# One Strassen level in the down product, and a causal convolution as three half-length filters, in a hybrid decoder layer

## The chip, the cores and the metric

The kernel runs on one core of one Trainium2 chip. The metric is the device time of one execution in microseconds (us); the time before is the median of three runs.

A core has TensorE (PE in the profile; its weight loads are PEld), VectorE (DVE), ScalarE (ACT), GpSimd (POOL) and SyncE (SP), which here only issues DMA transfers. Each engine works through its own queue in a fixed order.

## What is computed

One decoder layer on 2048 tokens of 1024 channels. After a first projection, half of the channels go through a sparse attention and half through a causal depthwise convolution; their normalised outputs are mixed into h, and a SwiGLU network follows. In the reference, with what the change does not touch left out:

```python
D_MODEL, SEQ, CONV_CH, CONV_WIDTH, FFN_HIDDEN = 1024, 2048, 512, 31, 2816

def conformer_conv(u, w_dw, b_dw, ln_g, ln_b):
    a, gate = jnp.split(u, 2, axis=-1)
    hcv = a * jax.nn.sigmoid(gate)
    hcv = lax.conv_general_dilated(hcv, w_dw, window_strides=(1,), padding=[(CONV_WIDTH - 1, 0)],
                                   feature_group_count=CONV_CH) + b_dw
    ...

hn = rms_norm(x, ffn_norm_g[l])
g_ff, u_ff = jnp.split(hn @ w_gate_up[l], 2, axis=-1)
x = x + (jax.nn.silu(g_ff) * u_ff) @ w_down[l]
```

## The kernel before, in words

Large products are made in float16 with both operands split into a high and a low part, so that one logical product is three matmuls: high x high, high x low and low x high. A split takes ScalarE (scale and cast to the high part) and then VectorE (scale, subtract the high part, cast).

**Convolution.** In the first phase, `conv` (L441) makes the gated input `hc` of one block of 128 channels and 1024 tokens, with 30 tokens of the block before it ahead, and puts 31 taps on a list. There are 8 such convolutions (4 channel blocks x 2 halves of the tokens). `tap` (L307) takes one from the list: a tap is one VectorE operation on 128x1024 elements, the first L317, the others L320, and all 31 add into the same tile `acc`. `mm3`, which issues the matmuls of the projection, takes a tap each time that it has streamed PACE = 3600 columns, and makes the tap wait for that matmul; what is left is worked off at the end of the half.

**Gate-up.** `ffn` (L1209) does gate and up in one Strassen level of its own: for each half `b` of the tokens (1024 each) and each chunk `j` of 128 hidden channels (22 chunks), `up` makes 7 products of 12 matmuls, 128x128 by 128x512. The weights' combinations s1, s2, s3 (`sm`) are made on GpSimd (L1394, L1395, L1402, L1415) and split by `wsplit` (L1349, L1350); the operands from the tokens are made in the first step of a half (L1315, L1316, L1327, L1329, L1334). Each chunk has one scale: ScalarE squares its weights (`chunk_norm`, L1249), a small matmul sums over partitions, and `root` (L1262) takes the power on GpSimd. The results go through tanh (L1378, ScalarE), a product (L1379, VectorE) and a second product (L1380, GpSimd), are squared for the scale of the activations (L1369, ScalarE), and are stored to HBM by SyncE as `act`.

**Down.** Four blocks `tb` of 512 tokens are each multiplied by all of w_down: for each of the 22 chunks one activation tile and one weight tile of 512 KB are loaded, split in three pairs (L1462 and L1463 for the activations, L1467 and L1468 for the weights), and 4 x 2 x 3 matmuls (L1475 to L1477) add into 8 PSUM banks. At the end of a block VectorE adds the residual h (L1483) and SyncE stores.

The order of the work on each engine is set by a scheduler from the order of the code and the tiles' buffers; taps have a low priority.

Of the kernel before, what the change touches and what calls it, by code (L numbers as in the profile page):

```python
# [25 lines left out]
NJ = HID // 128  # L26
CW = 31
EPS = 1e-6
# [19 lines left out]
PACE = (3600, 3600, 3600, 3600)  # L48
# [14 lines left out]
TAP0 = 0  # L63
# [30 lines left out]
class Body:  # L94
# [25 lines left out]
    def scratch(self):  # L120
        for name, w in (("qkv", 1048), ("mixc", 512), ("hd", D)):
            setattr(self, name, [self.dr.tile([128, w], F32, name=f"{name}{i}") for i in range(NT)])
        self.xt = [self.dr.tile([128, KT, 512], F32, name=f"xt{i}") for i in range(4)]
        self.act = [self.dr.tile([128, T], F32, name=f"act{j}") for j in range(NJ)]

# [181 lines left out]
    def tap(self, after=None):  # L307
        nc = self.nc
        w, acc, hc, j = self.taps.pop(0)
        with self.tc.high_priority(-LOWP):  # L310
            if w == 0:
                b0 = self.col["conv_dw_b"] + j
                if TAP0:
                    i = nc.scalar.activation(acc, hc[:, 0:1024], AF.Identity, scale=self.wdw[:, 0, j:j + 1],
                                             bias=self.vec[:, b0:b0 + 1])
                else:
                    i = nc.vector.tensor_scalar(acc, hc[:, 0:1024], self.wdw[:, 0, j:j + 1], self.vec[:, b0:b0 + 1],  # L317
                                                op0=ALU.mult, op1=ALU.add)
            else:
                i = nc.vector.scalar_tensor_tensor(acc, hc[:, w:w + 1024], self.wdw[:, w, j:j + 1], acc,  # L320
                                                   op0=ALU.mult, op1=ALU.add)
        if after is not None:
            self.tc.add_manual_dep(i.ins, after.ins.name,
                                   mybir.DependencyInfo(mybir.DependencyClass.Sync, mybir.DependencyReason.DATA),
                                   reason="taps keep pace with the matrix products")

# [4 lines left out]
    def phase_A_body(self, pb, ctx, ctx0):  # L331
# [23 lines left out]
        halo = sa.tile([128, 4, CW - 1], F32, name="halo")  # L355
        nc.vector.memset(halo, 0.0)
        kct = s0.tile([128, 4, 8, 129], F32, name="kct")
# [83 lines left out]
        def conv(j, x2, w2, between):  # L441
            hc = sa.tile([128, 1024 + CW - 1], F32, name="hc", tag="hc", bufs=HCB)
            nc.vector.tensor_copy(hc[:, :CW - 1], halo[:, j, :])
            for h in range(2):
                p = colmm(0, x2[h], w2)
                between(2 * h)
                t = s0.tile([128, 512], F32, name="sg", tag="sg", bufs=1)
                nc.scalar.activation(t, p, AF.Tanh, scale=w2[3])
                p = colmm(128, x2[h], w2)
                between(2 * h + 1)  # L450
                hv = hc[:, CW - 1 + h * 512:CW - 1 + (h + 1) * 512]
                nc.scalar.activation(hv, p, AF.Copy, scale=w2[2])
                nc.vector.scalar_tensor_tensor(hv, t, 1.0, hv, op0=ALU.add, op1=ALU.mult)
            nc.vector.tensor_copy(halo[:, j, :], hc[:, 1024:])
            acc = sa.tile([128, 1024], F32, name="acc", tag="acc", bufs=4)
            for w in range(CW):
                self.taps.append((w, acc, hc, j))
# [751 lines left out]
    def ffn(self, last, close_c):  # L1209
        nc, tc, I = self.nc, self.tc, self.I  # L1210
        with ExitStack() as ctx:
            sb = ctx.enter_context(tc.tile_pool(name="sbF", bufs=1, reuse_waits="tile"))
            ps = ctx.enter_context(tc.tile_pool(name="psF", bufs=1, space=PSUM, reuse_waits="tile"))
            self.xp = (ps, "pt", 2)
            self.hpool, self.htag = sb, ("wr", 6, "ev", EVB)
            wsc = sb.tile([128, 3, NJ], F32, name="wsc")
            ass = sb.tile([128, 2, 2 * NJ], F32, name="ass")
            dss = sb.tile([128, NJ], F32, name="dss")
            fin = sb.tile([128, 8], F32, name="fin")
            ssum = sb.tile([128, 3], F32, name="ssum")  # L1220
            one = sb.tile([128, 1], F32, name="one")
            nc.vector.memset(one, 1.0)
            sac = sb.tile([128, 2, NJ], F32, name="sac")
# [22 lines left out]
            def chunk_norm(ws):  # L1246
                ss = sb.tile([128, 2], F32, name="css", tag="css", bufs=2)
# [4 lines left out]
            def root(s, cols, pool=False):  # L1252
                if pool:
                    nc.gpsimd.partition_all_reduce(cols, cols, 128, bass.bass_isa.ReduceOp.add)
# [298 lines left out]
```

## Time and profile before

| | |
|---|---|
| runs (us) | 2837.37, 2833.8, 2825.53; median 2833.8 |
| the profiled execution | 2831.96 us, of it the profile's span 2830.2 us |
| mean granted TensorE clock | 0.96 |
| TensorE / VectorE / ScalarE / GpSimd busy | 2544.5 / 2030.0 / 1468.4 / 1020.0 us |
| convolution and projection | about 0 to 700 us of the span |
| attention and mixing | about 700 to 1480 us |
| gate-up, first and second half of the tokens | about 1480 to 1940, 1940 to 2370 us |
| down | about 2358 to 2830 us |

The shares of busy time are averages over stages with different limits, so the table by stage and the waits of one stage tell more than the page's first section. The granted clock is a share of TensorE's full 2.4 GHz. A matmul's duration in the profile (379 ns at full clock) is longer than the distance between two starts, since matmuls are pipelined.

### The profile page before, as it was taken

How to read it: one execution, taken by the hardware profiler on the slowest of the kernel's cores; microseconds unless marked ns; L12 is line 12 of the kernel's file. 1: busy time of each engine (PE TensorE's matmuls, PEld its weight loads, DVE VectorE, ACT ScalarE, POOL GpSimd, SP SyncE). 2: the span in 40 equal slices, each digit the busy share in tenths (PEclk: the TensorE clock that was granted, in tenths of full speed). 3: DMA queues.
4: the chain of work that ended last, by engine and by line, in shares of the span. 5: the costliest groups of instructions: out<-in, count | busy, mean ns of one | idle time of the engine just before them, and what ended most of it. 6: DMA issues, size and time to landing. Idle time of an engine off the chain costs nothing. (4 is left out here: it accounts for less than half of the span.)

```text
span 2830.2 us, 46376 instructions
## 1 busy us (share of the span) xinstructions
PE 2544.5 (90%) x17692; PEld 1547.2 (55%) x17692; DVE 2030.0 (72%) x3291; ACT 1468.4 (52%) x3101; POOL 1020.0 (36%) x903
## 2 busy tenths in 40 slices
PE   6987977666889988999987999997999999999999
PEld 3476446545677777777873444443444444444444
DVE  4899798889999898988767666668655556444442
ACT  7434632477667665655565555555544445433331
POOL 1001354545444443333455545547444441000000
PEclk9999988878999999999998999999999999999999
DMA  6124221113211111000025323333433225466452
GB/s 214 53 79 132 69 62 53 56 54 109 67 63 48 44 46 32 31 28 28 27 72 179 101 79 97 113 104 123 138 118 93 81 88 191 144 215 218 153 172 67
DMA packets 236088, 271.76 MB, mean 96 GB/s; under 512 B 18192, under 2 KB 172232, under 8 KB 235864
## 3 DMA queue, kind: packets, MB, share of 16 engines
q1 hardware_dynamic: 235616, 268.70, 29.8%
q8 instruction: 138, 2.26, 0.3%
q14 instruction: 86, 0.70, 0.1%
q10 hardware_dynamic: 248, 0.09, 0.0%
HBM read 207.73 MB, written 61.01 MB: 95 GB/s over the span
## 5 line engine op out<-in xcount | busy, mean ns | idle before, releaser
L1357 PE MATMUL ps<-oph,wh 128*128 128x512 f16 x1232 | 469.7, 381 | 33.6 <-DVE u L1405 10.9
L1359 PE MATMUL ps<-oph,wl 128*128 128x512 f16 x1232 | 470.1, 382 | 3.9 <-DVE wl L1350 3.8
L1360 PE MATMUL ps<-opl,wh 128*128 128x512 f16 x1232 | 470.1, 382 | 2.1 <-DVE opl L1316 1.8
L320 DVE SCALAR_TENSOR_TENSOR acc<-hc,wdw,acc 128x1024 f32<-128x1024 f32 x240 | 330.1, 1388 | 10.6
L1056 ACT ACTIVATE mp<-s,few 128x512 f32<-128x512 f32 x412 | 269.2, 691 | 108.7 <-PE s L1048 74.6
L1066 POOL TENSOR_TENSOR mpl<-mp 128x512 f16<-128x512 f32 x206 | 228.8, 1113 | 238.6 <-ACT mp L1056 235.9
L1468 DVE SCALAR_TENSOR_TENSOR wl<-wr,fin,wh 128x512 f16<-128x512 f32 x176 | 126.6, 750 | 240.9 <-ACT wh L1467 240.7
L1006 DVE TENSOR_REDUCE bx<-pp 128x8 f32<-128x512 f32 (+1 forms) x426 | 274.8, 664 | 20.9 <-PE pp L1003 19.2
L1467 ACT ACTIVATE wh<-wr,fin 128x512 f16<-128x512 f32 x176 | 121.8, 719 | 275.2 <-PE pt L1476 273.9
L1359 PEld LDWEIGHTS <-wl 128*128 128x128 f16 x1232 | 120.9, 98 | 179.4 <-issue 35.3
L1046 PE MATMUL s<-r,k 128*128 128x256 f16 x824 | 211.4, 277 | 1.8 <-ACT mp L1056 1.3
L1048 PE MATMUL s<-r,k 100*128 100x256 f16 x824 | 212.3, 278 | 0.0
L1079 PE MATMUL uu<-v,mp 128*128 128x129 f16 x1648 | 205.5, 224 | 3.6 <-ACT us L1102 3.5
L1357 PEld LDWEIGHTS <-wh 128*128 128x128 f16 x1232 | 122.8, 100 | 156.8 <-ACT wh L1349 6.8
L1360 PEld LDWEIGHTS <-wh 128*128 128x128 f16 x1232 | 121.2, 98 | 146.7 <-issue 3.6
L1475 PE MATMUL ps<-wh,ah 128*128 128x512 f16 x528 | 200.1, 379 | 0.0
L1476 PE MATMUL ps<-wl,ah 128*128 128x512 f16 x528 | 200.1, 379 | 0.0
L1477 PE MATMUL ps<-wh,al 128*128 128x512 f16 x528 | 200.1, 379 | 0.0
L1079 PE MATMUL uu<-v,mpl 128*128 128x65 f16 x1648 | 189.6, 196 | 4.6 <-POOL mpl L1066 2.4
L1380 POOL TENSOR_TENSOR t<-t,c 128x512 f32<-128x512 f32 x88 | 142.5, 1620 | 120.1 <-DVE t L1379 110.6
L1066 DVE TENSOR_TENSOR mpl<-mp 128x512 f16<-128x512 f32 x206 | 162.9, 795 | 31.7 <-ACT mp L1056 31.2
L1003 PE MATMUL pp<-k,r 128*128 128x512 f16 (+3 forms) x544 | 163.0, 340 | 10.8 <-DVE bx L1006 9.0
(343 smaller groups left out, 6480.6 us busy)
## 6 DMA issues: line engine op xcount, KB each, us to landing
wr<-in_w_gate_up_dram SPq DMA_DIRECT2D x88, 512.0 KB, 3.8
wr<-in_w_down_dram SPq DMA_DIRECT2D x88, 512.0 KB, 4.4
act<-t SPq DMA_DIRECT2D x88, 256.0 KB, 2.1
a<-act SPq DMA_DIRECT2D x88, 256.0 KB, 5.4
raw<-in_w_in_dram SPq DMA_DIRECT2D x44, 256.0 KB, 3.9
wn<-in_w_down_dram SPq DMA_DIRECT2D x22, 512.0 KB, 3.6
x<-in_x_dram SPq DMA_DIRECT2D x16, 512.0 KB, 3.5
h<-in_x_dram SPq DMA_DIRECT2D x16, 512.0 KB, 3.7
```

Of the source, the lines that this page charges most:

```text
L320: i = nc.vector.scalar_tensor_tensor(acc, hc[:, w:w + 1024], self.wdw[:, w, j:j + 1], acc, op0=ALU.mult, op1=ALU.add)
L1006: nc.vector.tensor_reduce(bx[:, h0:h0 + per, 2 * (ka - k0):2 * (kb - k0)], mp.rearrange("p h (b x) -> p h b x", x=64), axis=AX.X, op=ALU.max)
L1046: nc.tensor.matmul(s[:, i], self.k1[br][:, g, ks], r1[:, h0:h0 + 2, :], start=i % 2 == 0, stop=False, skip_group_check=True)
L1048: nc.tensor.matmul(s[:, i], self.k2[br][:KAUG, g, ks], r2[:KAUG, h0:h0 + 2, :], start=False, stop=base is None, skip_group_check=True)
L1056: nc.scalar.activation(p32[:, :n], s[:, :n], AF.Exp, scale=self.kap[:, job[0][0]:job[0][0] + 1])
L1066: eng.tensor_tensor(pl[:, :n], p32[:, :n], ph[:, :n], op=ALU.subtract)
L1079: nc.tensor.matmul(uu[:, hh, :n], w[:, i, hh, :], self.v[br][:, self.slot(br, kt), g, :n], start=new, stop=last and n == 129, skip_group_c ...
L1357: nc.tensor.matmul(p, wh[:, k, :], xh[:, k, :], start=start and k == 0, stop=False, skip_group_check=True)
L1359: nc.tensor.matmul(p, wl[:, k, :], xh[:, k, :], start=False, stop=False, skip_group_check=True)
L1360: nc.tensor.matmul(p, wh[:, k, :], xl[:, k, :], start=False, stop=stop and k == 3, skip_group_check=True)
L1475: nc.tensor.matmul(p, ah[:, k, ts], ws[c][0], start=j == 0, stop=False)
L1476: nc.tensor.matmul(p, ah[:, k, ts], ws[c][1], start=False, stop=False)
```

## The change

**Down.** One Strassen level (Winograd's form): per half `b` of the tokens, w_down and the activations are cut in 2 x 2 blocks, 7 products of 11 k-steps x 4 row blocks x 3 matmuls are made, and sums of them give the four blocks of the output. The activations' sums S1 to S4 are made on GpSimd in gate-up (`combine`) and stored beside the blocks A11, A12 and A22. To that end gate-up walks its chunks in pairs (j, j + 11) that share one scale, with weights loaded two chunks ahead. The weights' sums T1 to T4 are made on GpSimd in `down` (`operand`), from float32 tiles that stay in SBUF for the half. The first three k-steps of the first product are split before gate-up ends (`early`). The last pair's stores go through GpSimd's queue (`store`), and the scale of the second half's activations is summed by a small matmul.

**Convolution.** Even and odd samples of `hc` are kept apart (read from PSUM with a stride of two). A filter of the even taps on the even samples (16 operations), one of the odd taps on the odd samples (15) and one of the summed taps on the summed samples (16) give the even outputs as the sum of the first two and the odd outputs as the third less both; 3 more operations make the sums. That is 50 operations on 512 to 527 elements in place of 31 on 1024. PACE is 2232 columns.

```diff
-PACE = (3600, 3600, 3600, 3600)
+PACE = (2232, 2232, 2232, 2232)
...
+        def even(i):
+            ev = tile("ev", 512) if i == 0 else t["ev"]
+            if i == 0:
+                return nc.vector.tensor_scalar(ev, x0[:, :512], h(0), self.vec[:, b0:b0 + 1], op0=ALU.mult, op1=ALU.add)
+            return stt(ev, x0[:, i:i + 512], h(2 * i), ev, op0=ALU.mult, op1=ALU.add)
...
+        def odd(i):
+            x = x1[:, i - 1:i + 512]
+            if i == 1:
+                return nc.vector.tensor_scalar(tile("fq", 513), x, h(1), None, op0=ALU.mult)
+            return stt(t["fq"], x, h(2 * i - 1), t["fq"], op0=ALU.mult, op1=ALU.add)
...
+        def cross(i):
+            x = t["fx"][:, i:i + 512]
+            if i == 0:
+                return stt(tile("od", 512), x, g(0), t["fp"], op0=ALU.mult, op1=ALU.subtract)
+            return stt(out[:, 1] if i == HALF else t["od"], x, g(i), t["od"], op0=ALU.mult, op1=ALU.add)
+
+        steps = [lambda i=i: even(i) for i in range(HALF + 1)] + [lambda i=i: odd(i) for i in range(1, HALF + 1)]
+        steps.append(lambda: tt(tile("fx", 512 + HALF), x0, x1, op=ALU.add))
+        steps.append(lambda: stt(tile("fp", 512), t["ev"], self.nb2[:, j:j + 1], t["fq"][:, 1:], op0=ALU.add, op1=ALU.add))
+        steps.append(lambda: tt(out[:, 0], t["ev"], t["fq"][:, :512], op=ALU.add))
+        return steps + [lambda i=i: cross(i) for i in range(HALF + 1)]
...
-                nc.scalar.activation(hv, p, AF.Copy, scale=w2[2])
+                hv = hc[:, :, HALF + h * 256:HALF + (h + 1) * 256]
+                nc.scalar.activation(hv, p.rearrange("p (m e) -> p e m", e=2), AF.Copy, scale=w2[2])
...
+            order = [j for i in range(NH2) for j in (i, i + NH2)]
+            ahead_w = [load_w(order[0]), load_w(order[1])]
             src = load_x(0)
...
-            chunk_scale(0, chunk_norm(nxt))
+            chunk_scale(0, chunk_norm(ahead_w[0] + ahead_w[1]))
...
+            def store(name, b, p, t):
+                last = b == 1 and p == NH2 - 1 and name not in ("A11", "S3")
+                (nc.gpsimd if last else nc.sync).dma_start(self.act[name][b][p], t)
+
+            def combine(b, j):
+                tt, p = nc.gpsimd.tensor_tensor, j % NH2
+                if j < NH2:
+                    a11, a21 = kept[j]
+                    s3 = at()
+                    tt(s3, a11, a21, op=ALU.subtract)
+                    store("S3", b, p, s3)
+                else:
+                    (a11, a21), (a12, a22) = kept.pop(p), kept.pop(j)
+                    tt(a21, a21, a22, op=ALU.add)
+                    store("S1", b, p, a21)
+                    tt(a11, a21, a11, op=ALU.subtract)
+                    store("S2", b, p, a11)
+                    s4 = at()
+                    tt(s4, a12, a11, op=ALU.subtract)
+                    store("S4", b, p, s4)
...
                 s3 = sm()
                 tt(s3, a11, a21, op=ALU.subtract)
+                flush(sums)
                 product(pb, wsplit(s3, j), src, ops, "T3", False, True)
...
+                if name == "T2":
+                    tt(b11, b12, b11, op=ALU.subtract)
+                    t2 = tile("t2", 3)
+                    tt(t2, b22, b11, op=ALU.subtract)
+                    return t2
...
+                if name == "T3":
+                    tt(b12, b22, b12, op=ALU.subtract)
+                    return b12
...
+                if name == "T4":
+                    t2 = tile("t2", 3)
+                    tt(t2, b22, b11, op=ALU.subtract)
+                    tt(b21, b21, t2, op=ALU.subtract)
+                    return b21
...
+            def product(p, a, name, start, stop):
+                for k in K:
+                    if b == 0 and a == "A11" and k < len(early):
+                        blocks[0, 0, k] = early[k][0]
+                        (ah, al), (wh, wl) = early[k][1:]
+                    else:
+                        x = tile("ar", 6)
+                        nc.sync.dma_start(x, self.act[a][b][k])
+                        ah, al = split("a", x, sac[:, b, k:k + 1])
+                        wh, wl = split("w", operand(name, k), sd)
+                    for i in range(4):
+                        ts = slice(i * 128, i * 128 + 128)
+                        s = start and k == 0
+                        nc.tensor.matmul(p[i], ah[:, ts], wh, start=s, stop=False, skip_group_check=True)
+                        nc.tensor.matmul(p[i], ah[:, ts], wl, start=False, stop=False, skip_group_check=True)
+                        nc.tensor.matmul(p[i], al[:, ts], wh, start=False, stop=stop and k == NH2 - 1,
+                                         skip_group_check=True)
...
+            product(pa, "A11", "B11", True, True)
...
+            if b == 0:
+                act_scale(root)
...
+            product(pb, "S2", "T2", True, True)
+            u2 = plus(pb, p1)
+            h = residual(0, 0)
+            product(pa, "A12", "B21", False, True)
+            result(0, 0, pa, h)
+            product(pb, "S3", "T3", False, True)
+            u3 = plus(pb, p1)
+            with_h(u3, 1, 1)
+            with_h(p1, 1, 0)
+            pc = [bank() for _ in range(4)]
+            product(pc, "S1", "T1", True, True)
+            result(1, 1, pc, u3)
+            with_h(u2, 0, 1)
+            product(pb, "A22", "T4", False, True)
+            result(1, 0, pb, p1)
+            product(pc, "S4", "B22", False, True)
+            result(0, 1, pc, u2)
```

The order of the instructions shows three places. The first is GpSimd's queue at the seam from gate-up to down. Before, the last products t*u (L1380) are followed only by the sum over partitions for the activation scale (ISA rows, then the power at L217), and GpSimd has no part in down:

```order
856 L1380 TENSOR_TENSOR t<-t,c_27531 128x512
857 L1380 TENSOR_TENSOR t<-t,c_27513 128x512
858 L1254 ISA
859 L1254 ISA ssum<-ssum 128x1
860 L215 ISA
861 L215 TENSOR_SCALAR fin<-ssum 128x1
862 L217 TENSOR_TENSOR fin<-fin,mhalf 128x1
```

Now (t*u is L1440 with the tile `at`; L1417 are the stores, L1428, L1430 and L1433 the sums S1, S2 and S4, L1294 the power of the scale, L1569, L1571 and L1576 the weights' differences for T1, T2 and T3, of which this triple stands eleven times in a row for the first half):

```order
930 L1440 TENSOR_TENSOR at<-at,c_28013 128x512
931 L1417 DMA A_176<-at 128x512
932 L1440 TENSOR_TENSOR at<-at,c_27995 128x512
933 L1417 DMA A_198<-at 128x512
934 L1428 TENSOR_TENSOR at<-at 128x512
935 L1417 DMA S_220<-at 128x512
936 L1430 TENSOR_TENSOR at<-at 128x512
937 L1417 DMA S_242<-at 128x512
938 L1433 TENSOR_TENSOR at<-at 128x512
939 L1417 DMA S_286<-at 128x512
940 L1294 TENSOR_TENSOR fin<-fin,mhalf 128x1
941 L1569 TENSOR_TENSOR ew_27705<-wf,ew_27705 128x512
```

Five stores and three sums have come between the last t*u and the power of the scale, and the weights' differences follow it.

The second place is GpSimd's queue in a steady step of gate-up. Before (L1380 is t*u, L1394, L1395, L1402 and L1415 the weights' combinations s1, s2, s3 and the last one):

```order
582 L1380 TENSOR_TENSOR t<-t,c_20715 128x512
583 L1394 TENSOR_TENSOR sm<-wr 128x512
584 L1395 TENSOR_TENSOR sm<-sm,wr 128x512
585 L1380 TENSOR_TENSOR t<-t,c_20689 128x512
586 L1402 TENSOR_TENSOR sm<-wr 128x512
```

Now, in the step after the second chunk of a pair (t*u is L1440, s1 to s3 are L1456, L1457 and L1464):

```order
599 L1440 TENSOR_TENSOR at<-at,c_21382 128x512
600 L1456 TENSOR_TENSOR sm<-wr 128x512
601 L1457 TENSOR_TENSOR sm<-sm,wr 128x512
602 L1440 TENSOR_TENSOR at<-at,c_21354 128x512
603 L1428 TENSOR_TENSOR at<-at 128x512
604 L1430 TENSOR_TENSOR at<-at 128x512
605 L1464 TENSOR_TENSOR sm<-wr 128x512
606 L1433 TENSOR_TENSOR at<-at 128x512
607 L1478 TENSOR_TENSOR sm<-wr,sm 128x512
```

S1 and S2 stand between the second t*u and s3; S4 stands behind s3. In the step after a pair's first chunk it is S3 alone.

The third place is VectorE's queue among the taps. Before (L432 splits the projection's weights):

```order
137 L432 SCALAR_TENSOR_TENSOR wl<-raw,wsc,wh 128x1024 x3
138 L320 SCALAR_TENSOR_TENSOR acc<-hc,wdw,acc 128x1024 x9
139 L317 TENSOR_SCALAR acc<-hc,wdw,vec 128x1024
140 L443 COPY hc<-halo 128x30
141 L320 SCALAR_TENSOR_TENSOR acc<-hc,wdw,acc 128x1024 x2
```

Now, at the like place (L467 is the same split; `od`, `ev` and `fq` are the running sums of the three filters, `fx` the summed samples):

```order
163 L467 SCALAR_TENSOR_TENSOR wl<-raw,wsc,wh 128x1024 x2
164 L348 SCALAR_TENSOR_TENSOR od<-fx,wsum,od 128x512 x13
165 L348 SCALAR_TENSOR_TENSOR acc<-fx,wsum,od 128x512
166 L335 TENSOR_SCALAR ev<-hc,wdw,vec 128x512
167 L351 TENSOR_TENSOR fx<-hc 128x527
168 L336 SCALAR_TENSOR_TENSOR ev<-hc,wdw,ev 128x512 x5
```

The operations are half as long and more in number. Of 248 before, 164 stand right behind an operation that writes the same tile, and 84 behind another one; of 400 now it is 224 and 176.

## Rows read from the trace of the kernel before

**Rows 1.** The page: engines' busy time, and the taps' group (x count, busy, mean ns).

```profile
PE 2544.5 (90%) x17692; PEld 1547.2 (55%) x17692; DVE 2030.0 (72%) x3291; ACT 1468.4 (52%) x3101; POOL 1020.0 (36%) x903
...
L320 DVE SCALAR_TENSOR_TENSOR acc<-hc,wdw,acc 128x1024 f32<-128x1024 f32 x240 | 330.1, 1388 | 10.6
```

**Rows 2.** The page: the chain that ended last, by line.

```profile
PE ps L1475 4%; PE ps L1477 4%; PE ps L1476 4%; PE ps L1357 2%; PE ps L1359 2%; PE ps L1360 2%; PE pt L1475 1%; PE pt L1476 1%; PE pt L1477 1%; DVE h L1483 0%; POOL t L1380 0%; POOL sm L1394 0%; DVEq L1549 0%; ACT t L1378 0%; ACT wh L1349 0
```

**Rows 3.** Table by stage: busy us and instructions of each engine, granted clock, DMA.

```profile
core 0: us, PE busy (x) PEld busy (x) DVE busy (x) ACT busy (x) POOL busy (x), PEclk, DMA share, GB/s
0.00:700.00 700.00, 547.18 (x3702) 370.37 (x3703) 586.73 (x779) 363.10 (x854) 227.32 (x216) 0.90 0.28 88
...
1480.00:1520.00 40.00, 25.07 (x138) 16.62 (x139) 25.25 (x37) 20.41 (x39) 21.84 (x19) 0.74 0.70 228
1520.00:1560.00 40.00, 31.00 (x137) 13.63 (x136) 33.76 (x42) 18.43 (x34) 25.43 (x19) 0.91 0.54 167
...
1940.00:1980.00 40.00, 24.82 (x98) 10.07 (x97) 39.66 (x41) 20.79 (x39) 32.23 (x21) 0.88 0.37 115
2020.00:2358.00 338.00, 337.81 (x1569) 153.32 (x1567) 191.32 (x269) 160.37 (x281) 149.18 (x112) 1.00 0.32 98
2358.00:2830.00 472.00, 468.09 (x2169) 212.05 (x2167) 208.72 (x307) 175.98 (x269) 5.38 (x5) 1.00 0.51 169
...
2400.00:2500.00 100.00, 100.00 (x465) 45.30 (x463) 46.05 (x68) 39.34 (x60) 0.00 (x0) 1.00 0.60 197
```

**Rows 4.** TensorE's waits, 0 to 700 us and 1480 to 1560 us (us, times, longest).

```profile
PE pp L194 <- DVE vsc L191: 16.1, 1, 16.1
...
PE x L580 <- DVE acc L320: 10.5, 2, 10.1
...
PE x L249 <- DVE h L1177: 7.8, 1, 7.8
```

**Rows 5.** VectorE's timeline near 100 us, then taps: min/median/max ns.

```profile
101.20 2.47 DVE L432 SCALAR_TENSOR_TENSOR wl<-raw,wsc,wh 128x1024 f16<-128x1024 f32 x2
103.59 12.38 DVE L320 SCALAR_TENSOR_TENSOR acc<-hc,wdw,acc 128x1024 f32<-128x1024 f32 x9
...
L320 DVE SCALAR_TENSOR_TENSOR acc<-hc,wdw,acc x240: 1162/1283/2715, 63.9 to 574.3; 128x1024 f32<-128x1024 f32 x120
...
L317 DVE TENSOR_SCALAR acc<-hc,wdw,vec x8: 801/806/811, 62.9 to 520.4; 128x1024 f32<-128x1024 f32 x8
```

**Rows 6.** Single lines: duration ns min/median/max, first and last start.

```profile
L1467 ACT ACTIVATE wh<-wr,fin x176: 704/722/722, 2357.8 to 2810.4; 128x512 f16<-128x512 f32 x176
...
L1468 DVE SCALAR_TENSOR_TENSOR wl<-wr,fin,wh x176: 740/747/1051, 2358.7 to 2811.1; 128x512 f16<-128x512 f32 x176
...
L1398 DVE TENSOR_TENSOR u<-ps,p x44: 676/682/693, 1519.9 to 2357.4; 128x512 f32<-128x512 f32 x44
...
L1380 POOL TENSOR_TENSOR t<-t,c x88: 1264/1712/1790, 1545.5 to 2374.4; 128x512 f32<-128x512 f32 x88
```

**Rows 7.** DMA: issues with KB each, median us to landing; one issue on SyncE.

```profile
act<-t SPq DMA_DIRECT2D x88, 256.0 KB, 2.1
a<-act SPq DMA_DIRECT2D x88, 256.0 KB, 5.4
...
1489.35 0.58 SPq L1169 DMA_DIRECT2D h<-in_x_dram  x1
```

**Rows 8.** TensorE's longest wait in total, 1520 to 1940 us.

```profile
PE ps L1357 <- ACT p L1392: 9.8, 20, 0.6
```

**Rows 9.** Timeline of GpSimd, then of ScalarE, in a steady step of gate-up.

```profile
2213.44 1.27 POOL L1402 TENSOR_TENSOR sm<-wr 128x512 f32<-128x512 f32 x1
2216.47 1.27 POOL L1415 TENSOR_TENSOR sm<-wr,sm 128x512 f32<-128x512 f32 x1 [1.76 <-DVE wl L1350]
2221.50 1.26 POOL L1394 TENSOR_TENSOR sm<-wr 128x512 f32<-128x512 f32 x1 [3.76 <-DVE wl L1350]
...
2219.91 0.72 ACT L1349 ACTIVATE wh<-sm,wsc 128x512 f16<-128x512 f32 x1 [1.93 <-PE ps L1359]
```

**Rows 10.** Timeline of ScalarE, then of VectorE, at the FFN's start.

```profile
1487.38 1.04 ACT L1249 ACTIVATE junk<-wr 128x1024 bf16<-128x1024 f32 x1
...
1489.07 11.33 DVE L1316 TENSOR_TENSOR opl<-src,oph 128x512 f16<-128x512 f32 x8 [1.90 <-ACT oph L1315]
```

More of the change, by code (lines that the diff above doesn't have):

```diff
@@ L62 @@
 MTB = 1
-TAP0 = 0
 F12 = 16
@@ L308, in tap @@
         nc = self.nc
-        w, acc, hc, j = self.taps.pop(0)
         with self.tc.high_priority(-LOWP):
[L311 to L321, printed above, removed]
+            i = self.taps.pop(0)()
         if after is not None:
@@ L1384, in up @@
+                kept.setdefault(i // 2, []).append(t)
+                if i != 2 * (i // 2) + 1 or i // 2 >= NH2:
+                    store(("A11", None, "A12", "A22")[i % 2 + 2 * (i // 2 // NH2)], b, i // 2 % NH2, t)
             def up(b, j, src, ops, ws, ahead, scales):
@@ new lines, in up, with ahead, scales @@
+                silu_mul(u2, c22, b, 2 * j + 1)
+                sums.append(lambda: combine(b, j))
+            steps = [(b, j) for b in range(2) for j in order]
+            for n, (b, j) in enumerate(steps):
+                if n % NJ == 0:
+                    ops = {}
+                if n + 2 < len(steps):
+                    ahead_w.append(load_w(steps[n + 2][1]))
+                if n == NJ - 1:
+                    nsrc = load_x(1)
+                held = []
+                def ahead():
+                    if n + 2 < NJ and n % 2:
+                        held.append(chunk_norm(ahead_w[1] + ahead_w[2]))
+                    if n == 2 * NJ - 1:
+                        for e, k in zip(early, range(3)):
+                            for x, c in ((e.pop(), sac[:, 0, k:k + 1]), (e[0], fin[:, 0:1])):
+                                hi, lo = (keep.tile([128, 512], F16, name="eh", tag="eh", bufs=12) for _ in "hl")
+                                nc.scalar.activation(hi, x, AF.Copy, scale=c)
+                                nc.vector.scalar_tensor_tensor(lo, x, c, hi, op0=ALU.mult, op1=ALU.subtract)
+                                e.append((hi, lo))
+                    if NJ // 2 <= n < NJ + NJ // 2:
+                        down_norm(n - NJ // 2)
+                def scales():
+                    if held:
+                        chunk_scale((n + 1) // 2, *held)
+                    if n == NJ + 12:
+                        down_scale()
+                        act_scale(0, temp())
+                if n == 2 * NJ - 2:
+                    early = []
+                    for k in range(3):
+                        x = keep.tile([128, 512], F32, name="ea", tag="ea", bufs=1)
+                        w = keep.tile([128, 512], F32, name=f"ew{k}")
+                        nc.sync.dma_start(x, self.act["A11"][0][k])
+                        self.load_down(wd, 0, 0, k, w)
+                        early.append([w, x])
+                up(b, j, src if n % NJ == 0 else None, ops, ahead_w[0], ahead, scales)
+                ahead_w.pop(0)
+                for _ in last:
+                    pass
+                if n == NJ - 1:
+                    src = nsrc
```

232 lines of the change are left out of this document (129 added, 103 removed).

## The prediction, made before the changed kernel was run

> **What bounds the kernel now.** I read the page first [rows 1]: TensorE is busy for 90% of the span, VectorE for 72%, GpSimd for 36%. Next the chain that ended last [rows 2]: its rows are the matmul lines of the down product (L1475 to L1477) and of gate-up (L1357 to L1360), so the end of the program hangs on TensorE alone. Then the table by stage [rows 3], because the averages hide three regimes. In the down stage (2358 to 2830 us) TensorE works 468.09 of 472 us at the full granted clock (1.00, its 2.4 GHz level) and GpSimd does almost nothing. Gate-up in its second half (2020 to 2358) is just as solid: 337.81 of 338 us. The start of the FFN (1480 to 1520) and the switch between the halves (1940 to 1980) have TensorE at 25 of 40 us. In the first 700 us, projection and convolution, TensorE works 547 us and VectorE 587. There the matmuls wait for VectorE in several places, one of them the taps themselves [rows 4], and VectorE's taps run back to back [rows 5]. So time comes out of this kernel where TensorE does fewer matmuls in a solid stage, or VectorE does less before 700 us.
>
> **The down product: fewer matmuls.** Before: 4 token blocks x 22 chunks x 8 x 3 = 2112 matmuls. After: 2 halves x 7 products x 11 x 4 x 3 = 1848. In a stretch without waits 465 matmuls start in 100 us [rows 3], 0.215 us each. 264 fewer are **-56.8 us**. Nothing else in the old stage bounds it, so all of this lies on the path. Per 12 matmuls (2.58 us) the new loop splits two tiles: 0.72 us on ScalarE and 0.75 us on VectorE each [rows 6], so 1.5 of 2.58 us. Before it was three splits per 24. Both fit.
>
> **The seam from gate-up to down.** The last five stores and the root of the activation scale now stand on GpSimd's queue, behind three combinations. After the last gate-up matmul come VectorE's sum, tanh on ScalarE and VectorE's product, about 2.1 us at 0.7 each [rows 6]; then on GpSimd t*u, S1, S2 and S4 at 1.26 to 1.72 [rows 6], 5.1 to 6.9; five DMA issues, which no row shows on GpSimd: one SyncE issue took 0.58 [rows 7], so 2.9; then scale and split on VectorE, 1.3. That is 11.4 to 13.2 us. TensorE has only 36 matmuls (3 k-steps, split early) to bridge it, 7.8 us, and k=3 needs the scale. **+5 us**; 1 if issues cost GpSimd nothing, 10 if each takes 1.6. While TensorE waited at 1480 to 1520 its granted clock was 0.74 and 0.91 in the 40 us behind [rows 3]; for a shorter hole I take **+2** (0 to 4).
>
> Next comes product T2, whose right operand GpSimd builds from w_down: three subtractions per k in the first half (b11, t2, b12, in that order in its queue), against 2.58 us of matmuls. Uncontended 3 x 1.27 = 3.8 us, contended 3 x 1.71 = 5.1. I take 4.2, since VectorE has two splits per k there where gate-up kept it over half busy. The first weights land about 22 us after gate-up's end: A-side loads wait for the six-deep ring, freed by splits that start near 13, and a load lands 5.4 us after issue [rows 7]. T2's last operand is then ready at 22 + 11 x 4.2 - 1.4 = 67, its matmuls end at 67 + 4 = 71. Without the wait T2 would end at 7.8 + 5 + 20.7 + 28.4 = 62. **+9 us**; 5 at 3.8, 19 at 5.1. T3 and T4 are built by then. In the second half GpSimd is done with the first half's builds some 55 us ahead, so T2 there has cover; without it, 9 more. The tail (four VectorE evictions of 0.74 and a store) is the old one. DMA moves about 80 MB in 410 us, 195 GB/s; the old stage ran 100 us at 197 GB/s with no wait [rows 3].
>
> **Gate-up.** Chunks go in pairs that share a scale, so the root comes every second step. The first half now waits 20 times at L1357 for p1, 9.8 us in all [rows 8]; with half the norms I take **-5** (0 to -8). New are 88 combinations on GpSimd. In steady gate-up GpSimd finished s3 at 2214.7 and ScalarE split it at 2219.9, when a slot came free [rows 9]: 5.2 us of slack. S1 and S2 now stand before s3: 2.5 to 3.4 us. It fits, S4 follows in gaps of 1.8 and 3.8 us [rows 9], and the price is **0**. If the slack were gone, each us over it would cost 22 us (below). At the FFN's start ScalarE squares four weight tiles instead of two (1.05 us each) ahead of the operand splits, which VectorE and then TensorE's 7.8 us wait hang on [rows 4, 10]; another 1 MB is loaded first: **+3** (0 to 5). At the switch VectorE is busy 39.66 of 40 us [rows 3]; three combinations enter GpSimd's queue there: **+2** (0 to 5).
>
> **The convolution.** 248 operations of 1024 elements become 400 of 512 to 527 (368 like the tap, 16 like the first, 16 additions). A 1024 tap takes 1.283, a 512 operation of the same kind 0.747 [rows 5, 6]: halving the length saves 42%, not 50%, since about 0.21 us do not depend on length. A dependent tap starts 1.376 us after the last (12.38 us for nine), so 0.10 more; one behind an unrelated operation about 0.08 less. In VectorE's order 164 of the old and 224 of the new operations follow their own predecessor. Before: 240 x 1.283 + 8 x 0.81 + 164 x 0.10 - 84 x 0.08 = 324. After: 368 x 0.747 + 16 x 0.55 + 16 x 0.69 + 224 x 0.10 - 176 x 0.08 = 303. So -21 us of VectorE, of which I put 0.6 on the path, where VectorE and TensorE take turns: **-12 us**. Bounds: if time went by elements (25,600 of 31,744 per convolution), 0.19 x 340 = -64; if contention (the tap's mean of 1388 against the median of 1283 [rows 1, 5], 0.105 us) fell on each operation alike, 152 x 0.105 = +16 on top, near zero. The stride of two in PSUM reads (32 on ScalarE, half idle there) and in 16 VectorE writes has no row; at double time for the 16 writes, +9.
>
> **Sum.** -56.8 + 5 + 2 + 9 - 5 + 3 + 2 - 12 = -52.8 us against the profiled execution's 2832.0: 2779.2. The median of the runs is 1.8 above that execution: **2781 us**.
>
> **Rivals.**
> - *GpSimd and VectorE shut each other out.* L1380 has median 1.712, minimum 1.264 [rows 6]; a tap once took 2.715 [rows 5], 1.43 more than its median, about a whole GpSimd operation. If each build loses a whole split, T2 runs at 3 x 1.27 + 2 x 0.75 = 5.3 us per k: T2 ends at 22 + 58.3 - 1.8 + 4 = 82.5, +20 instead of +9, and the seam 2 more: 2794. Against it: the usual loss in L1380 is 0.45, not 0.75. Chance 0.18. The Trainium skill ("SBUF — State Buffer", section "SBUF: two separate sides") states just this: a VectorE operation with two SBUF inputs and a GpSimd operation that reads SBUF take the shared port as an exclusive lock, the second waiting the first out. The median loss of 0.45 us agrees with such waits in part, as a second operation seldom arrives just when the first starts.
> - *Taps by elements.* If long taps are bound by data rather than by issue, VectorE sheds 64 us, 0.6 of it on the path: 26 more, 2755. Against: 0.747 is not half of 1.283. Chance 0.10.
> - *The convolution gains nothing*, or the strided writes eat it: +12 to +20, 2797. Chance 0.16.
> - *Slower: the combinations push s3 past its slot.* Place: the second step of each pair, 22 times. S1 and S2 stand before s3; beyond 5.2 us together each us costs 22. At 4.5 us each (one blocked behind a store that must land first, 2.1 us [rows 7], and a contended neighbour) it is 3.8 x 22 = 84, so 2865. It brings no change from 3.8 us each and decides beyond 4.0; the longest such operation in the trace was 1.79 [rows 6], so chance 0.06.
> - *The matmuls go and the time stays.* If the down loop waits for GpSimd or for loads in both halves and through T3 and T4 too, at 3.8 us instead of 2.58 for four products of eleven steps, 44 x 1.2 = 53 us are given back: 2825. For it: in the old stage GpSimd was idle, so no row shows this loop under it. Against: two of the four have builds finished ahead. Chance 0.08.
>
> **Numbers.** The rest, 0.42, is the forecast, between 2768 and 2794 by its own small terms. The range runs from 2752 (taps by elements) to 2820, which leaves out slower, part of "time stays" and the far end of the element case. About 0.5%, 14 us, is what a measurement of this kernel tells from no change: faster 0.86, same 0.08 (the case at 2825), slower 0.06.
>
> **What would show it.** Right: a down stage of 415 to 425 us with 1848 matmuls at 0.215; TensorE's two largest waits there at k=3 (for wl, behind GpSimd's root) and in T2 for t2; none in the second half. In gate-up, waits as before. Taps of 512 near 0.75 with 303 to 330 us in all, and the first 700 us shorter by 10 to 15. Wrong: waits on s3 or S1 in every second step, builds over 5 us per k, or the convolution's VectorE time not below its present one.

## The result, and the profile after

The change takes 2800.7 us (median of 4 runs, 2796.9 to 2804.6) against 2832.4 before (4 runs): a ratio of 0.989, 95% interval 0.9864 to 0.9915, so 31.7 us faster. The forecast was 2781, with a range up to 2820: the sign was right and the time is in the range, but of 51 us forecast 32 came.

The page after, first section, and the table by stage (same columns as [rows 1] and [rows 3]):

```profile
PE 2502.0 (89%) x17430; PEld 1529.1 (55%) x17430; DVE 2189.0 (78%) x3463; ACT 1508.2 (54%) x3153; POOL 1317.8 (47%) x1117
```

```profile
core 0: us, PE busy (x) PEld busy (x) DVE busy (x) ACT busy (x) POOL busy (x), PEclk, DMA share, GB/s
2363.00:2400.00 37.00, 30.27 (x131) 13.29 (x130) 22.79 (x28) 16.45 (x27) 22.34 (x20) 0.91 0.92 314
2400.00:2480.00 80.00, 64.89 (x288) 27.83 (x286) 63.52 (x50) 35.56 (x56) 72.76 (x47) 1.00 0.54 172
2480.00:2600.00 120.00, 120.00 (x558) 54.41 (x557) 96.33 (x115) 62.14 (x94) 38.54 (x25) 1.00 0.78 261
2600.00:2700.00 100.00, 96.26 (x443) 43.05 (x442) 98.33 (x86) 50.58 (x78) 70.24 (x43) 1.00 0.42 123
2700.00:2796.00 96.00, 95.49 (x443) 43.07 (x441) 64.89 (x80) 42.19 (x64) 19.27 (x12) 1.00 0.35 110
```

The old down stage was solid [rows 3]; the new one has holes up to 2480 us and again between 2600 and 2700, just where GpSimd is busy. Between 2600 and 2700 VectorE is busy 98% of the time with only 86 instructions.

To see where the 30.6 us of span came from, I set marks in both traces: the end of VectorE's last tap, and TensorE's last matmul of the attention, its first of gate-up, and its first and last of down.

| | before | after | difference |
|---|---|---|---|
| last tap ends | 576 | 553 | -22 |
| attention ends | 1478.9 | 1469.3 | -9.6 |
| FFN's start (to gate-up's first matmul) | 32.4 | 39.1 | +6.7 |
| gate-up | 858.8 | 855.4 | -3.4 |
| down (first to last matmul) | 455 | 431 | -24 |

The taps after (group, busy us and mean ns, 0 to 700 us; the three filters' main lines) beside [rows 1, 5]:

```profile
L336 DVE SCALAR_TENSOR_TENSOR ev<-hc,wdw,ev 128x512 f32<-128x512 f32 x120 | 99.7, 831 | 7.5 <-PE mm L253 0.5
L348 DVE SCALAR_TENSOR_TENSOR od<-fx,wsum,od 128x512 f32<-128x512 f32 x112 | 98.7, 882 | 10.4 <-PE mm L253 4.3
L342 DVE SCALAR_TENSOR_TENSOR fq<-hc,wdw,fq 128x513 f32<-128x513 f32 x112 | 86.1, 769 | 7.8
```

With the seven smaller groups the 400 operations last 323 us in sum, against 340 for the old 248 (240 of 1.388 and eight of 0.8 us); with overlaps counted once it is 318 against 336.

TensorE's waits in down (us, times, longest), and its longest wait at the FFN's start:

```profile
PE acc L1601 <- DVE wl L1553: 20.5, 21, 6.7
PE acc L1600 <- ACT wh L1552: 5.1, 5, 1.0
...
PE x L251 <- DVE h L1211: 13.9, 1, 13.9
```

Of down's 25.6 us, 6.7 are at the seam. T2's product (the first two rows below, 2400 to 2440 us) waits 8.3. The product behind it, A12 with the block B21 as loaded, waits 6.8 (the third row, 2440 to 2480 us), though its right operand is no sum. The last 3.7 are in the second half, 3.1 of them again in A12 with B21:

```profile
PE acc L1600 <- ACT wh L1552: 5.1, 5, 1.0
PE acc L1601 <- DVE wl L1553: 3.2, 5, 0.6
...
PE acc L1601 <- DVE wl L1553: 6.8, 9, 2.2
```

Under T2's product GpSimd's three builds per k follow one another without a break, 4.57 us per k (rows one to four), and the chain that ended last follows them from 2391 to 2436 us. Under the next product GpSimd already builds T4 (L1582 and L1583), and each of VectorE's splits takes 1.75 us (the last four rows):

```profile
2414.52 1.71 POOL L1569 TENSOR_TENSOR wf<-wf 128x512 f32<-128x512 f32 x1
2416.31 1.60 POOL L1571 TENSOR_TENSOR t<-wf 128x512 f32<-128x512 f32 x1
2417.86 1.27 POOL L1576 TENSOR_TENSOR wf<-wf 128x512 f32<-128x512 f32 x1
2419.09 1.72 POOL L1569 TENSOR_TENSOR wf<-wf 128x512 f32<-128x512 f32 x1
...
2444.20 1.61 POOL L1582 TENSOR_TENSOR t<-wf 128x512 f32<-128x512 f32 x1
2445.76 1.72 POOL L1583 TENSOR_TENSOR wf<-wf,t 128x512 f32<-128x512 f32 x1
...
2444.59 1.76 DVE L1553 SCALAR_TENSOR_TENSOR al<-ar,sac,ah 128x512 f16<-128x512 f32 x1
2446.28 1.75 DVE L1553 SCALAR_TENSOR_TENSOR wl<-wf,fin,wh 128x512 f16<-128x512 f32 x1
```

GpSimd's timeline at the seam and in the first builds for T2:

```profile
2366.30 1.26 POOL L1440 TENSOR_TENSOR at<-at,c 128x512 f32<-128x512 f32 x1 [1.75 <-DVE at L1439]
2367.87 0.58 POOL L1417 DMA_DIRECT2D A<-at  x1 [0.31 <-POOL at L1440]
...
2374.94 0.57 POOL L1294 TENSOR_TENSOR fin<-fin,mhalf 128x1 f32<-128x1 f32 x1
2386.59 1.29 POOL L1569 TENSOR_TENSOR ew<-wf,ew 128x512 f32<-128x512 f32 x1 [11.08 <-DMA wf<-in_w_down_dram]
...
2391.18 1.72 POOL L1569 TENSOR_TENSOR ew<-wf,ew 128x512 f32<-128x512 f32 x1
2392.98 1.59 POOL L1571 TENSOR_TENSOR t<-wf,ew 128x512 f32<-128x512 f32 x1
2394.54 1.72 POOL L1576 TENSOR_TENSOR wf<-wf 128x512 f32<-128x512 f32 x1
2396.21 1.71 POOL L1569 TENSOR_TENSOR ew<-wf,ew 128x512 f32<-128x512 f32 x1
```

A store on GpSimd holds its queue for 0.9 us (0.31 of waiting for the sum, 0.58 of issue); the power of the scale starts at 2374.9. The three builds of one k take 5.0 us here and settle at 4.6.

### The profile page after: what moved, and what is told of

It reads as the page before. It is cut to its first block, busy times and chain, and to the rows that moved or that the text cites. A ratio compares the mean times of both kernels' runs of the same rounds, so it can differ in the third digit from the quotient of the medians.

```text
span 2799.6 us, 46901 instructions
## 1 busy us (share of the span) xinstructions
PE 2502.0 (89%) x17430; PEld 1529.1 (55%) x17430; DVE 2189.0 (78%) x3463; ACT 1508.2 (54%) x3153; POOL 1317.8 (47%) x1117
## 5 line engine op out<-in xcount | busy, mean ns | idle before, releaser
L1601 PE MATMUL acc<-wl,ah 128*128 128x512 f16 x604 | 229.8, 380 | 20.5 <-DVE wl L1553 20.5
L1600 PE MATMUL acc<-wh,ah 128*128 128x512 f16 x604 | 229.8, 380 | 5.1 <-ACT wh L1552 5.1
L1602 PE MATMUL acc<-wh,al 128*128 128x512 f16 x604 | 229.9, 381 | 0.0
L1382 ACT ACTIVATE wh<-sm,wsc 128x512 f16<-128x512 f32 x176 | 125.8, 716 | 148.2 <-PE ps L1392 146.4
L1383 DVE SCALAR_TENSOR_TENSOR wl<-sm,wsc,wh 128x512 f16<-128x512 f32 x176 | 182.5, 1038 | 25.7 <-ACT wh L1382 25.7
L1383 DVE SCALAR_TENSOR_TENSOR wl<-wr,wsc,wh 128x512 f16<-128x512 f32 x132 | 142.4, 1079 | 69.4 <-ACT wh L1382 68.3
L1552 ACT ACTIVATE ah<-ar,sac 128x512 f16<-128x512 f32 x151 | 108.6, 719 | 162.6 <-PE acc L1601 157.4
L1553 DVE SCALAR_TENSOR_TENSOR al<-ar,sac,ah 128x512 f16<-128x512 f32 x151 | 160.4, 1062 | 45.8 <-ACT ah L1552 45.8
```

The costliest lines, as they stand in the source:

```text
L1383: nc.vector.scalar_tensor_tensor(lo, x, sw, hi, op0=ALU.mult, op1=ALU.subtract)
L1600: nc.tensor.matmul(p[i], ah[:, ts], wh, start=s, stop=False, skip_group_check=True)
L1601: nc.tensor.matmul(p[i], ah[:, ts], wl, start=False, stop=False, skip_group_check=True)
L1602: nc.tensor.matmul(p[i], al[:, ts], wh, start=False, stop=stop and k == NH2 - 1, skip_group_check=True)
```

## The experiments

Differences in time are to the runs of before that were taken beside each kernel; the change itself is at -31.7.

**1. Each half alone.** e1_conv is the kernel before with the diff's convolution, e2_down the kernel before with the rest of the diff:

```diff
 e1_conv, of the change's diff only
-PACE = (3600, 3600, 3600, 3600)
+PACE = (2232, 2232, 2232, 2232)
...
-            for w in range(CW):
-                self.taps.append((w, acc, hc, j))
+            self.taps += self.filters(hc, acc, j)
```

> The new convolution alone, with gate-up and down as before. In the change the last tap ends 22 us earlier, but the attention behind it takes 13 us longer. Theory (the attention's longer time comes with the convolution, by the order that the scheduler then gives the attention): last tap near 553 us, end of the attention near 1469, time 8 to 11 us below before. Rival (the attention pays for the new FFN's loads and weights that share its end): end of the attention near 1457, time 20 us below before.

> The new gate-up and down alone, with the convolution as before. Theory (down gives 25 us, the FFN's start costs 7, gate-up gives 3): 20 to 23 us below before, attention as long as before. Rival (the attention's 13 us belong to the FFN): 8 to 10 us below before.

Measured: e1_conv 2817.8 (ratio 0.9957, 0.9944 to 0.9969; -13.9), e2_down 2807.4 (0.9925, 0.9911 to 0.9938; -24.3). In e1_conv the last tap ends at 554 and the attention at 1470.7, 8.2 before the old end; in e2_down the attention lasts 877 us, from its first to its last matmul into `uu`, as before (878), in e1_conv 892, as in the change (891). So the attention's 13 us come with the convolution, and TensorE's order in it agrees: its 8528 matmuls from the first to the last into `uu` follow one another in the same order, by tiles and shapes, in before and e2_down, and in the change and e1_conv, while the two pairs differ in 1660 places. TensorE's granted clock is not what differs: it was 0.95 on average over the attention in before, and 0.95 in e4_sp_stores (below), where the attention has the change's order and takes 888 us. By its runs e1_conv gained 3 us more than the upper end expected, e2_down 1 more; e1_conv's profiled span lies 10 below that of before. One profile tells an end only to some 4 us: in e2_down, whose convolution is the old one, the attention ends at 1475.0, 3.9 before that of before. The halves' gains add up to 38.2 us by the runs and 34.5 by the spans, the change's are 31.7 and 30.6: no more apart than this scatter. FFN start and down behave as the parts say: 37 and 431 us in e2_down, 30 and 455 in e1_conv.

**2. GpSimd's third build.** 

```diff
                 if name == "T3":
-                    tt(b12, b22, b12, op=ALU.subtract)
+                    i = tt(b12, b22, b12, op=ALU.subtract)
+                    tc.add_manual_dep(i.ins, last_t2[0].ins.name, ...)
```

> The change with one dependence more: the builds of T3 (b12) stand behind all builds of T2 in GpSimd's queue, two per k in place of three. Theory (T2's wait in the first half is GpSimd's third operation): T2's builds take 3.2 us per k instead of 4.8, TensorE's waits between 2400 and 2480 us fall from 15 to under 3, time 13 to 16 us below the change. Rival (VectorE's splits under contention, or the loads, set T2's pace): waits stay over 8 us, under 6 us gained.

Measured: 2794.8 (0.9874, 0.9861 to 0.9887; -36.9), down 4.6 us shorter than in the change, 21.8 us of waits in down where the change has 25.6. The theory held for T2 and fell for the time. The builds for T2 did take 3.3 us per k, and T2's product (2398 to 2426 us) no longer waits at all. But TensorE waits 11.2 us in the products behind it, from 2426 to 2480, where the change has 6.8. The table of e3_t3_late (in T2's product, then in A12 with B21), and a piece of its timeline in the latter, VectorE and then GpSimd, show why:

```profile
2395.00:2415.00 20.00, 20.00 (x95) 9.03 (x94) 20.00 (x13) 10.31 (x16) 19.53 (x13) 1.00 0.85 288
...
2435.00:2455.00 20.00, 14.55 (x66) 6.16 (x65) 20.00 (x16) 6.67 (x10) 19.69 (x13) 1.00 0.55 176
```

```profile
2442.65 1.75 DVE L1553 SCALAR_TENSOR_TENSOR al<-ar,sac,ah 128x512 f16<-128x512 f32 x1
2444.32 1.75 DVE L1553 SCALAR_TENSOR_TENSOR wl<-wf,fin,wh 128x512 f16<-128x512 f32 x1
2445.99 1.75 DVE L1553 SCALAR_TENSOR_TENSOR al<-ar,sac,ah 128x512 f16<-128x512 f32 x1
...
2442.14 1.71 POOL L1587 TENSOR_TENSOR wf<-wf,t 128x512 f32<-128x512 f32 x1
2443.93 1.59 POOL L1586 TENSOR_TENSOR t<-wf 128x512 f32<-128x512 f32 x1
2445.49 1.71 POOL L1587 TENSOR_TENSOR wf<-wf,t 128x512 f32<-128x512 f32 x1
```

Both engines go in step: 13 operations of each in the first 20 us, one VectorE split ending per GpSimd sum, each split in the timeline 1.75 us long where it takes 0.75 alone [rows 6]. Two splits per k are then 3.3 us, more than the k-step's 2.58 us of matmuls. GpSimd is building T4 there, long before T4 is needed. With T2 relieved of one operation, VectorE was the next in line.

**3. No weight sums at all.** e7_no_build makes none of the 110 sums; for T2, and likewise for T3 and T4:

```diff
                 if name == "T2":
-                    tt(b11, b12, b11, op=ALU.subtract)
-                    t2 = tile("t2", 3)
-                    tt(t2, b22, b11, op=ALU.subtract)
-                    return t2
+                    return b12
```

> The change without any of the weights' sums T1 to T4 (the raw blocks are multiplied instead, so the output is another one); the same loads, splits and matmuls. Theory: VectorE's splits in down take 0.75 us instead of 1.06 on average, TensorE waits only at the seam, down lasts 408 to 412 us instead of 431. Rival (splits are slowed by the loads' traffic): splits stay at 1 us and waits remain in the first half.

Measured, in a single run: 2775.5 us, down 408.1 us. TensorE's waits in down, and the splits of the weights (ns min/median/max):

```profile
PE acc L1594 <- DVE wl L1553: 7.0, 1, 7.0
...
L1553 DVE SCALAR_TENSOR_TENSOR wl<-wf,fin,wh x148: 739/745/1758, 2375.3 to 2755.3; 128x512 f16<-128x512 f32 x148
```

The same loads and splits, and only the seam's wait is left: the sums on GpSimd cost down 23 us, in both halves together.

**4. The sums spread out.** e6_paced moves the products to the order A11, A12, S2, S1, S3, A22, S4 (T2 is needed third, not second), forms T4 in place, moves the loads of the weights' blocks along with this, and ties each sum but T2's own to one k-step's last matmul:

```diff
+                if name == "B11":
+                    load(0, 1, k)
+                elif name == "B21":
+                    load(1, 1, k)
+                    behind(tt(b11, b12, b11, op=ALU.subtract), m)
+                elif name == "T2":
+                    behind(tt(b12, b22, b12, op=ALU.subtract), m)
+                elif name == "T1":
+                    behind(tt(b21, b21, b22, op=ALU.subtract), m)
+                elif name == "T3":
+                    behind(tt(b21, b21, b11, op=ALU.add), m)
```

> The change with the products of down in another order (A11, A12, S2, S1, S3, A22, S4), T4 formed in place (b21 - b22, later + T1), and each of GpSimd's weight sums tied to one k-step's last matmul, so that about one falls on each. Theory (while GpSimd adds without a pause, VectorE gets one split through per GpSimd operation, 1.55 us instead of 0.75, and 2 splits per k-step at 1.55 are slower than its 2.58 us of matmuls): with the sums spread out TensorE's waits in down, 25.6 us, fall under 10, the seam's 6.7 among them; time 12 to 18 us below the change. Rival (GpSimd's total work is too much for the stage however it lies): 0 to 6 us gained.

Measured: 2787.6 (0.9847, 0.9831 to 0.9863; -44.2), down 421.7 us, waits 17.6 us, 6.9 of them the seam's. A gain of 12 by the runs and 9 in down, but waits of 11 us remain where I wanted 3: spreading helps, and is not enough while GpSimd makes the sums.

**5. The sums on VectorE.** e9_dve_sums is e6_paced with all the weights' sums on VectorE, of which only T1's stay tied to a matmul; the additions of h stay on GpSimd:

```diff
-                    tt(t2, b22, b11, op=ALU.subtract)
+                    nc.vector.tensor_tensor(t2, b22, b11, op=ALU.subtract)
...
-                    behind(tt(b12, b22, b12, op=ALU.subtract), m)
+                    nc.vector.tensor_tensor(b12, b22, b12, op=ALU.subtract)
```

> The order of e6_paced, with the weights' sums of down on VectorE instead of GpSimd (110 operations of about 0.70 us; only the 24 additions of h stay on GpSimd). Theory (GpSimd and VectorE hold each other up, so that a sum on GpSimd costs VectorE as much as it would cost to make it there): splits 0.75 us, per half 154 x 0.66 + 55 x 0.7 + 24 x 0.74 = 158 us of VectorE in 200, TensorE waits at the seam and little else, down 410 to 415 us, time 16 to 21 us below the change and 3 to 8 below e6_paced. Rival (VectorE is short of time either way): T2's and T3's products still wait, no better than e6_paced.

Measured: 2781.3 (0.9826, 0.9812 to 0.9839; -51.2), down 410.0 us. Table by stage, 2390 to 2670 us, of the change and then of e9_dve_sums, then the latter's wait in down and its splits of T2:

```profile
2390.00:2670.00 280.00, 262.35 (x1199) 116.95 (x1198) 238.09 (x222) 137.10 (x209) 182.28 (x115) 1.00 0.61 198
```

```profile
2390.00:2670.00 280.00, 279.27 (x1294) 126.39 (x1293) 234.95 (x354) 146.76 (x224) 16.57 (x12) 1.00 0.63 206
```

```profile
PE acc L1614 <- DVE wl L1553: 7.8, 3, 6.6
...
L1553 DVE SCALAR_TENSOR_TENSOR wl<-t,fin,wh x22: 733/737/744, 2420.2 to 2645.0; 128x512 f16<-128x512 f32 x22
```

In the same 280 us VectorE of the change was busy for 238.1 us with 222 instructions; here it is busy for 235.0 with 354. VectorE makes the sums in the time in which it had waited for GpSimd.

**6. The seam.** In e4_sp_stores the last five stores go to SyncE:

```diff
-                (nc.gpsimd if last else nc.sync).dma_start(self.act[name][b][p], t)
+                nc.sync.dma_start(self.act[name][b][p], t)
```

> The change with the last pair's five stores on SyncE's queue instead of GpSimd's. Theory (the 6.7 us wait at the fourth k-step is GpSimd's queue ahead of the power of the scale: 4 operations and 5 issues with the time around them, some 0.9 us per store): the power starts about 2.5 us earlier, when the small sum's matmul behind the 36 early matmuls is done, the wait falls to 4 to 4.5 us, the time by 2 to 3. Rival (the wait is for loads or splits): 6 to 7 us as before.

Measured: 2799.7 (0.9887, 0.9873 to 0.9901; -32.1). The wait fell from 6.7 to 4.4 us as expected, but all waits of down together stayed (25.8 us): TensorE came to T2 earlier and waited there for GpSimd's builds, 10.9 us instead of 8.3. The cause was right and the gain nil, as another wait stood next. Even at the seam something else now comes last: ScalarE waits for a load of activations until 2370.3 us, while the power was done at 2368.3.

**7. The FFN's start.** In the change h's load leaves SyncE behind 20 others (timelines of SyncE, then of VectorE):

```profile
1468.61 8.93 SPq L1275 DMA_DIRECT2D wr<-in_w_gate_up_dram  x4
1477.58 12.66 SPq L1326 DMA_DIRECT2D src<-xt  x16
1490.61 0.33 SPq L1203 DMA_DIRECT2D h<-in_x_dram  x1
...
1496.74 0.88 DVE L1211 SCALAR_TENSOR_TENSOR h<-x,few,h 128x256 f32<-128x256 f32 x2 [5.46 <-DMA h<-in_x_dram]
```

e5_ffn_start swaps the loads with the steps that load h:

```diff
-            src = load_x(0)
             for _ in range(6):
                 next(last)
+            src = load_x(0)
```

> The change with the 16 loads of src put behind the load of h in the code, so that h leaves SyncE's queue ahead of them. Theory (TensorE's 13.9 us wait for h at the FFN's start comes from h's load standing behind 4 weight and 16 src loads): the wait falls under 5 us and the time by 5 to 8 us. Rival from the prediction (four squares ahead of the operand splits set the start): under 2 us gained.

Measured: 2799.1 (0.9887, 0.9874 to 0.9901; -32.5). The wait for h fell to 1.8 us, and gate-up's first matmul came after 26.1 us instead of 39.1; but gate-up then took 865.5 us instead of 855.4, with new waits for the operands' splits, whose loads now came last. The time is the rival's, under 2 us gained, though not by its cause. Which load stands in front decides which wait is seen; that the sum of both is what costs is shown, how to save it is not.

**8. The attention's order.**

```diff
-PACE = (2232, 2232, 2232, 2232)
+PACE = (1800, 1800, 1800, 1800)
```

> The change with PACE 1800 instead of 2232: taps are allowed earlier, the scheduler gives the attention another order. Theory (the attention's length follows the order of its instructions: 878 us with one order, 892 with the other): the attention takes another time again, somewhere between 875 and 900 us, and the convolution ends within 5 us of 553. Rival (the attention is held up by what the shorter convolution leaves behind): attention again 890 to 894 us.

Measured: 2796.3 (0.9873, 0.986 to 0.9887; -35.5). The attention lasts 882 us, so not 891: the theory's side. But the taps end at 533, 20 us earlier, not within 5, and the attention's end is only 4 us earlier than the change's: when the last tap ends says little. Over all runs the attention took 877 to 878 us in two kernels (old convolution), 888 to 892 in eight (PACE 2232) and 879 to 883 in four (PACE 1800). TensorE's order is the same within each of these three groups and differs between them (from the change to e8_pace1800 in 1308 of the 8528 places). That the order is the cause, and not what lies on VectorE when the attention begins, is not separated.

**9. All together.** e10_pool_all and e11_dve_all add the edits of 6 and 8 to e6_paced and e9_dve_sums; e12_later_loads is e11_dve_all with

```diff
-                if name == "B11":
-                    load(0, 1, k)
-                elif name == "B21":
+                if name == "B21":
+                    load(0, 1, k)
                     load(1, 1, k)
```

> e6_paced (sums on GpSimd) with the last five stores on SyncE and PACE 1800. Theory: with T2 no longer next in line the seam's shorter wait is kept this time (2 to 3 us), and the attention's order of e8_pace1800 gives 4: 2780 to 2783 us. Rival (the seam's gain is swallowed again): 2784 to 2787.

> e9_dve_sums with the last five stores on SyncE and PACE 1800. Theory, as the sum of the parts: 6 to 8 us below e9_dve_sums, about 2774 to 2778 us, and 3 to 8 us below e10_pool_all. Rival (parts overlap): within 2 us of e9_dve_sums or e10_pool_all.

> e11_dve_all with the loads of the blocks (0, 1), which no product needs before the third, moved behind those of A11. In e11_dve_all SyncE's queue issues the last stores, which wait for GpSimd's sums, until 2366 us, then nine weight loads between the first four activation loads, and TensorE waits 7.9 us at the seam for a load. Theory (the seam has become a matter of SyncE's queue): the wait falls to 5 to 6 us, the time by 2 to 3. Rival (the stores alone set it): no change within 1 us.

Measured: e10_pool_all 2785.1 (0.9836, 0.9822 to 0.9849; -47.5), e11_dve_all 2776.1 (0.9807, 0.9793 to 0.982; -56.4), e12_later_loads 2776.3 (0.9794, 0.978 to 0.9807; -59.1). e10_pool_all came out where its rival stood: its seam waits 7.9 us. e11_dve_all is 5 below e9_dve_sums (6 to 8 were expected) and 9 below e10_pool_all (3 to 8), so the gain of VectorE's sums holds in both settings. The seam in e11_dve_all and e12_later_loads, TensorE's longest wait in down of each:

```profile
PE acc L1613 <- ACT wh L1552: 7.9, 1, 7.9
```

```profile
PE acc L1612 <- ACT wh L1552: 5.0, 1, 5.0
```

With the stores on SyncE the loads of down stand behind stores that wait for GpSimd, so the seam waits for a load; with fewer loads ahead the wait falls by 2.9 us, and down by 1.4, as TensorE then waits 2.0 us for activations at the third product. In the time of the runs that can't be told from nothing. e11_dve_all and e12_later_loads beat both kernels: 25 to 27 us more gained than the change.

## Why the prediction was right, and where it was short

- **-56.8 for fewer matmuls**: right. 1848 matmuls at 0.215 us are 397 us; down without sums took 408, the rest being the seam.
- **Seam, +5 and +2**: 6.7 us for wl at k=3, behind GpSimd's power, as said. The granted clock was 0.91 between 2363 and 2400: behind the wait the matmuls start 0.43 us apart for a while, which costs 2.8 us. The 0.58 of an issue was right; that 0.3 us of waiting goes with each store was missing.
- **T2, +9**: 8.3 us in T2's product, with GpSimd's builds as the chain, as said; that the number came so near is luck. I had taken 4.2 us per k, on the ground that VectorE has only two splits per k there; it was 4.6, and with that the same sum gives +13. It was less because TensorE came to T2 4.5 us later, by the seam's 1.7 and the clock's 2.8.
- **The product behind T2, and the second half, both 0**: this step failed. A12 with B21 waits 6.8 us, and the second half 3.7. "T3 and T4 are built by then" and "T2 there has cover" looked at when the sums are ready, and not at what making them does to the splits: I treated the contention as a longer GpSimd operation, and not as a longer VectorE split. While GpSimd builds T4 without a pause, two splits take 3.3 us per k, against 2.58 of matmuls.
- **Gate-up, -5 + 2, and 0 for the combinations**: measured -3.4, but not by the step named. The first half's waits for p1 fell from 9.8 us to 1.1, as said, and in their place TensorE waits 8.6 us, 11 times, for u3's sum on VectorE (L1468), in every second step. What was gained lies where the half begins: the waits for the weights' first splits fell from 9.9 us to 3.4. Why they did is not shown. That the sum came near is luck. The second half is solid (1.4 us of waits from 2020 to 2350), so the slack before s3 held.
- **FFN's start, +3**: +6.7, by another cause. I named four squares instead of two; VectorE's operand splits were done at 1491 and it then waited 5.5 us for h, whose load stood behind 20 others on SyncE.
- **Convolution, -12**: right in size, -9.6 at the attention's end and -13.9 by e1_conv's runs, but by another way. VectorE's taps fell by 16 us in sum, or 18 with overlaps counted once, where I had 21. Of that not 0.6 came through: the last tap ends 22 us earlier, and the attention then takes 13 us longer, for which the prediction had no term. That the two leave about the forecast is luck. The means (769 to 882 ns) lie above the medians of 0.75, so contention is in it; but the bound by which it takes 0.1 us from each of 400 operations and leaves near nothing did not come.
- **The rivals**: "GpSimd and VectorE shut each other out" is what happened, at 0.18, and its 2794 was nearer than the forecast. Its sum was not right either: it priced the loss as whole splits on GpSimd's side (T2 at 5.3 us per k, +20), where 4.6 came, and had nothing for the splits of the other products, 10.5 us. The Trainium skill ("SBUF — State Buffer", section "SBUF: two separate sides") says that of a VectorE operation with two SBUF inputs and a GpSimd operation that reads SBUF the second waits until the first is done; experiments 2, 3 and 5 agree, with splits of 1.75 us beside GpSimd's sums and 0.74 without. The slower rival, s3 past its slot, did not occur, nor did the convolution's two, nor the one in which 53 us are given back.

Sum of the misses, from the marks: down gave 24.3 where the steps said 40.8, 16.5 short. Of these 2.5 are the seam's and 10.5 the waits put at nothing, T2's product gave 0.7 back, and the remaining 4 fit what stands behind each of the 26 waits, where the next matmul starts 0.38 us later instead of 0.22. FFN's start and the convolution were 3.7 and 2.4 short, gate-up 0.4 better: 22 us, which take the forecast of 52.8 to the span's 30.6.

## What to carry to other kernels

Before work is put on an idle GpSimd, look at what VectorE does in the same stretch: the idle time in the profile is only free if VectorE has slack for the time that it will lose, and here the same sums were cheaper on VectorE itself. Price a contended pair from both sides, as two operations in step, and compare that with the rate at which the consumer takes their results. And when a wait is shortened, look for what stands next behind it: three of the experiments (2, 6 and 7) removed or shortened the wait they aimed at and gained nothing or a third of it.

## What was unexpected in the hardware

While GpSimd sums two SBUF tiles without a pause, VectorE's split of 512 columns takes 1.75 us instead of 0.75, and GpSimd's sum 1.6 to 1.7 instead of 1.27: one of each per 1.55 to 1.7 us. A busy VectorE in the profile can so be a waiting one: 222 instructions filled 238 us in the change, 354 filled 235 us with the sums moved to it.
